# Keys of the first attention turned by 32-by-32 blocks on VectorE after a trip through DRAM

## The chip, the core and the metric

One NeuronCore of one Trainium2 chip runs the whole program. The metric is device microseconds of one execution, as the median of several runs; a profiled execution of the same program gives the trace. In the trace PE is TensorE (matmuls), PEld its weight loads, DVE is VectorE, ACT ScalarE, POOL GpSimd, and SP the engine whose queue issues all DMAs here. L539 is line 539 of the kernel.

## What is computed

One step of a two-layer streaming encoder over 640 rows: 512 rows of a new stream (four row tiles of 128) and 8 running streams with 16 new rows each (the fifth row tile). Only the first mixer, the forgetting attention, is touched:

```python
def fox_mixer(h, q_pos, past, w_in, b_f, w_out):
    proj = h @ w_in
    q, k, v, f_pre, gate = jnp.split(proj, [...], axis=-1)
    ...                                # 16 heads of 64
    logf = jax.nn.log_sigmoid((f_pre + b_f).astype(jnp.float32))
    ...                                # cached keys and values ahead of the new ones
    def block(qb, cqb, pq):
        s = jnp.einsum('bqhd,bkhd->bhqk', qb, k_all).astype(jnp.float32) * FOX_SCALE
        s = s + jnp.moveaxis(cqb, 1, 2)[..., None] - ck
        p = masked_softmax(s, mask).astype(v_all.dtype)
        return jnp.einsum('bhqk,bkhd->bqhd', p, v_all)
    ...
    return o @ w_out, (k, v, logf.astype(h.dtype))
```

The new keys are also outputs, row by row (fox_k_p for the 512 rows, fox_k_s for the 128). For the scores the head dimension has to lie on the partitions, so the keys are needed turned. Products run in a split form: each fp32 operand is a high and a low part (fp32r), and three products stand for one.

## The kernel before

The phases follow one another: first attention (to about 550 us of the span), cross attention, feed-forward, then latent attention, cross attention and feed-forward of the second layer.

In the first attention the 16 heads are worked off in eight pairs, pr = 0 to 7. Each pair's stage merges three lists of steps by their relative position (`merge`, L210): `prompt_list(pr)`, the attention of the 512 rows; `sample_list(pr)`, that of the running streams over their cached keys; and a `fill` list of projections for pairs to come. Keys and values are projected for four heads (two pairs, 256 columns) at a time, so `k_list(g)` with g = 0 to 3 runs four times: g = 0 beside `logf_list` and `q_list(0)` ahead of the first pair, g = 1, 2, 3 as the first part of the fill of pairs 1, 3 and 5, followed there by the out projection of the pair before (`out_list`: ten products of six matmuls of 512 columns, each added into X by VectorE at L332) and by `q_list(pr + 1)`.

`k_list(g)` (L522) loads 256 columns of weights, projects the five row tiles into PSUM (L204), and ScalarE copies each into `krow` (L550). `store` writes `krow` to the two outputs (L531, L532). `tr(j)`, once for each of the two pairs, turns 128 columns: four TensorE transposes into one PSUM bank for the 512 rows (L539), from which `evac_split` makes the high part on ScalarE (L222) and the low part on VectorE (L223), the tiles kT; and one transpose for the 128 rows (L543), which VectorE copies into `kn` (L544). `sample_list` takes from kn the new columns of each stream on POOL (L688). kT is read by the scores of the pair, L627: for a block of query rows six matmuls, two heads of 64 rows by the three products of the split, `qT` stationary.

The cached keys already take another way: `sample_list`'s `load` brings them in blocks (L684: four DMAs of 128 KB, one for each 32 of the 128 columns, in runs of 32 floats, 128 bytes) into `kr`, and VectorE's 32-by-32 block transpose (L692) makes the turned keys out of it.

The order of instructions on each engine's queue is not quite the order of the program. A planner in the framework lays them out when the program is built: by its own estimated times, an instruction whose operands it holds ready may stand ahead of an earlier one that still waits, and otherwise the program's order decides. On the chip each queue then runs strictly in that order. Buffers come from tagged pools: `pw` has four of 128x512 floats (scores, biases), PSUM has three of `mm` (products), two of `s` (scores), two of `t` (transposes), one of `o`; `mrow` has two and serves the memory projection late in the phase.

Of the kernel before, what the change touches and what calls it, by code (L numbers as in the profile page):

```python
# [9 lines left out]
F32 = mybir.dt.float32  # L10
# [8 lines left out]
P = 128  # L19
D = 1024  # L20
KD = D // P
NP = 512
NT = 640
TT = NT // P
# [68 lines left out]
def fox_mla_kernel(ctx: ExitStack, tc: tile.TileContext, I, O):  # L93
    nc = tc.nc
    V, A, G, S, T = nc.vector, nc.scalar, nc.gpsimd, nc.sync, nc.tensor
# [6 lines left out]
    drp = ctx.enter_context(tc.tile_pool(name="drp", bufs=1, space=DRAM))  # L102
# [5 lines left out]
    ident = cst[:, C_ID:C_TRI]  # L108
# [27 lines left out]
    def psum_t():  # L136
        return pat.tile([P, 512], F32, tag="t", name="ps_t", bufs=2)
# [72 lines left out]
    def merge(*lists):  # L210

        steps = [((i + 0.5) / len(l), n, i) for n, l in enumerate(lists) for i in range(len(l))]
        for _, n, i in sorted(steps):
            lists[n][i]()
# [5 lines left out]
    def evac_split(hi, lo, ps, scale=None):  # L220
        if scale is None:
            A.copy(hi, ps)  # L222
            V.tensor_tensor(lo, ps, hi.bitcast(F32), ALU.subtract)  # L223
        else:
            A.activation(hi, ps, AF.Copy, scale=scale)
            V.scalar_tensor_tensor(lo, ps, scale, hi.bitcast(F32), ALU.mult, ALU.subtract)
# [178 lines left out]
    def fox_phase():  # L405
# [8 lines left out]
        with ExitStack() as st:  # L414
# [5 lines left out]
            ckd = drp.tile([NH, NP], F32, name="ckd")  # L420
            csd = drp.tile([P, KS], F32, name="csd")
            lfd = drp.tile([P, NH], F32, name="lfd")
            Qbd = [fp.tile([P, B, 32], F32, name=f"Qbd{i}", bufs=1) for i in range(2)]

            def pw_tile():
# [96 lines left out]
            def k_list(g):  # L522
                c0 = 256 * g
                d = {}

                def load():
                    d["w"] = load_w([(0, 256, w_in[:, 1024 + c0:1024 + c0 + 256])])
                    d["row"] = fp.tile([P, TT, 256], F32, tag="krow", name="krow", bufs=1)

                def store():  # L530
                    S.dma_start(ko[:, :, c0:c0 + 256], d["row"][:, 0:TT - 1, :])  # L531
                    S.dma_start(kso[:, c0:c0 + 256], d["row"][:, TT - 1, :])  # L532

                def tr(j):
                    cs_ = slice(j * P, (j + 1) * P)
                    kT = [fp.tile([P, NP], F32R, tag=f"kT{i}", name=f"kT{i}", bufs=3) for i in range(2)]
                    pt = psum_t()
                    for t in range(TT - 1):
                        T.transpose(out=pt[:, t * P:(t + 1) * P], in_=d["row"][:, t, cs_], identity=ident)  # L539
                    evac_split(kT[0], kT[1], pt)  # L540
                    kn = fp.tile([P, P], F32, tag="kn", name="kn", bufs=3)
                    pt = psum_t()
                    T.transpose(out=pt[:, 0:P], in_=d["row"][:, TT - 1, cs_], identity=ident)  # L543
                    V.tensor_copy(kn, pt[:, 0:P])  # L544
                    ks[2 * g + j] = (kT, kn)

                L = [load]
                for t in range(TT):
                    L += gemm(lambda t=t: as_ops(nx.T, slice(t * P, (t + 1) * P), d["w"], slice(0, 256), KD), 256,
                              lambda ps, t=t: A.copy(d["row"][:, t, :], ps[:, 0:256]), parts=2)  # L550
                return L + [store, lambda: tr(0), lambda: tr(1)]

            def q_list(pr):
                c0 = P * pr
                Q = Qbd[pr % 2]
                d = {}

                def load_q():
                    d["q"] = load_w([(0, P, w_in[:, c0:c0 + P])], per=8)
                    qT = [fp.tile([P, NP], F32R, tag=f"qT{i}", name=f"qT{i}", bufs=2) for i in range(2)]  # L560
                    qs_[pr] = (qT, Q)

                def load_g():
                    d["g"] = load_w([(0, P, w_in[:, 3088 + c0:3088 + c0 + P])], per=8)
                    sg[pr] = fp.tile([P, NT], F32, tag="sig", name="sig", bufs=2)

                def done_q(ps, half):
                    qT = qs_[pr][0]
                    n = HALF if half == 0 else NP - HALF
                    evac_split(qT[0][:, half * HALF:half * HALF + n], qT[1][:, half * HALF:half * HALF + n],  # L570
                               ps[:, 0:n], FOX_SCALE)
                    if half == 1:
                        for hh in range(2):
                            A.activation(Q[64 * hh:64 * hh + 64, :, TS * hh:TS * hh + TS],
                                         ps[64 * hh:64 * hh + 64, n:HALF].rearrange("p (b t) -> p b t", t=TS),
                                         AF.Copy, scale=FOX_SCALE)

                def done_g(ps, half):
                    A.activation(sg[pr][:, half * HALF:(half + 1) * HALF], ps[:, 0:HALF], AF.Exp, scale=-1.0)

                def sig():
                    A.activation(sg[pr], sg[pr], AF.Ln, bias=1.0)
                    A.activation(sg[pr], sg[pr], AF.Exp, scale=-1.0)

                L = []
                for ld, nm, dn in ((load_q, "q", done_q), (load_g, "g", done_g)):
                    L.append(ld)
                    for half in range(2):
                        L += gemm(lambda nm=nm, half=half: ws_ops(d[nm], slice(0, P), nx.T,
                                                                  slice(half * HALF, (half + 1) * HALF), KD),  # L590
                                  HALF, lambda ps, dn=dn, half=half: dn(ps, half), parts=3)
                return L + [sig]
# [198 lines left out]
                    nx.all(t + 1)  # L791
                vl[1 + t]()
            vl[-1]()
            merge(logf_list(), k_list(0) + q_list(0))
            mems = mem_list(0, lambda: fp) + mem_list(1, lambda: fp)
            for pr in range(8):
                fill = []
                if pr % 2 == 1 and pr < 7:
                    fill += k_list(pr // 2 + 1)
                elif pr < 7:  # L800
                    fill += q_list(pr + 1)
                if 0 < pr < 7:
                    ld, tiles = out_list(pr - 1)
                    fill += [ld] + sum(tiles, [])
                if pr % 2 == 1 and pr < 7:
                    fill += q_list(pr + 1)
                if pr % 2 == 0 and pr < 6:
                    fill += v_list(pr // 2 + 1)
                if pr == 6:
                    fill += sum(mems[:4], [])  # L810
                if pr == 7:
                    fill += sum(mems[4:9], [])
                merge(prompt_list(pr), sample_list(pr), fill)
                finish(pr)
# [998 lines left out]
```

## Time and profile before

| | |
|---|---|
| median of three runs | 2077.21 us (2076.77 to 2082.59) |
| the profiled execution | 2078.31 us |
| its span, first to last instruction | 2076.5 us |
| mean granted TensorE clock | 0.996 |
| DMA packets over the span | 352123, 236.37 MB, 133444 of them under 512 bytes |
| TensorE idle in 40 to 360 us of the span | 320.00 - 314.79 = 5.2 us |

The profile page gives the busy share of each engine, the time in 40 slices, the DMA queues, the chain of work that ended last and the costliest groups of instructions. The trace can be asked further: by stretch of time, line or tile, for waits and for single instructions in order of time. A busy share is a mean over stages with different limits, so the page is read first and the stretch with the changed code after it. "Idle before" is the time an engine stood before an instruction, with what released it. Starts of matmuls are closer together than they are long, since they are pipelined.

### The profile page before, as it was taken

How to read it: one execution, taken by the hardware profiler on the slowest of the kernel's cores; microseconds unless marked ns; L12 is line 12 of the kernel's file. 1: busy time of each engine (PE TensorE's matmuls, PEld its weight loads, DVE VectorE, ACT ScalarE, POOL GpSimd, SP SyncE). 2: the span in 40 equal slices, each digit the busy share in tenths (PEclk: the TensorE clock that was granted, in tenths of full speed). 3: DMA queues.
4: the chain of work that ended last, by engine and by line, in shares of the span. 5: the costliest groups of instructions: out<-in, count | busy, mean ns of one | idle time of the engine just before them, and what ended most of it. 6: DMA issues, size and time to landing. Idle time of an engine off the chain costs nothing. (4 is left out here: it accounts for less than half of the span.)

```text
span 2076.5 us, 34659 instructions
## 1 busy us (share of the span) xinstructions
PE 2022.2 (97%) x13501; PEld 1809.6 (87%) x13501; DVE 1390.2 (67%) x2658; ACT 884.8 (43%) x1723; POOL 196.9 (9%) x398
## 2 busy tenths in 40 slices
PE   7999999999999999999999989999999999999998
PEld 7988888877987899999998978887987899999997
DVE  5455555655556896687687567777556886687686
ACT  4443344554343443343344455554343443343342
POOL 1222222220100000000002311100000000000000
PEclk9999999999999999999999999999999999999999
DMA  7565656477557332232221342113566332232221
GB/s 195 117 153 119 154 142 148 144 232 230 139 165 197 103 92 72 82 92 71 82 82 55 103 112 53 53 52 87 132 178 188 97 90 73 82 92 71 82 82 61
DMA packets 352123, 236.37 MB, mean 114 GB/s; under 512 B 133444, under 2 KB 316484, under 8 KB 351960
## 3 DMA queue, kind: packets, MB, share of 16 engines
q1 hardware_dynamic: 351960, 234.16, 40.4%
q8 instruction: 107, 1.75, 0.4%
q14 instruction: 56, 0.46, 0.1%
HBM read 216.90 MB, written 17.21 MB: 113 GB/s over the span
## 5 line engine op out<-in xcount | busy, mean ns | idle before, releaser
L204 PE MATMUL mm<-hT,whi 128*128 128x320 f32 x1744 | 288.6, 312 | 2.9 <-ACT hT L222 2.9
L204 PEld LDWEIGHTS mm<-hT,whi 128*128 128x128 f32 x1744 | 262.2, 190 | 8.4 <-ACT hT L222 4.3
L151 DVE TENSOR_TENSOR wlo<-raw,whi 128x1024 fp32r<-128x1024 f32 (+4 forms) x145 | 170.0, 1175 | 136.0 <-ACT whi L150 115.7
L332 DVE TENSOR_TENSOR X<-mm,X 128x512 f32<-128x512 f32 x270 | 183.0, 686 | 113.5 <-PE mm L204 111.9
L150 ACT CAST whi<-raw 128x1024 fp32r<-128x1024 f32 (+4 forms) x145 | 144.6, 1003 | 133.0 <-PE mm L204 64.9
L1154 ACT CAST whi<-tw 128x512 fp32r<-128x512 f32 (+1 forms) x120 | 91.9, 766 | 214.4 <-PE mm L204 127.8
L204 PE MATMUL mm<-whi,oT 128*128 128x512 f32 x544 | 178.6, 407 | 3.1 <-DVE X L332 1.7
L204 PE MATMUL mm<-whi,aT 128*128 128x512 f32 x560 | 173.0, 390 | 0.3 <-ACT aT L1119 0.3
L204 PE MATMUL mm<-hT,wlo 128*128 128x320 f32 x872 | 155.4, 312 | 0.0
L204 PEld LDWEIGHTS mm<-hT,wlo 128*128 128x128 f32 x872 | 133.5, 190 | 3.3 <-issue 3.2
L232 POOL TENSOR_SCALAR rstd<-ss 128x1 f32<-128x1 f32 x49 | 16.1, 328 | 1252.8 <-ACT hn L230 1248.4
L204 PE MATMUL mm<-s,whi 128*128 128x320 f32 x768 | 128.2, 309 | 0.0
L204 PE MATMUL mm<-whi,hT 128*128 128x256 f32 (+2 forms) x800 | 126.0, 296 | 0.2 <-ACT whi L150 0.2
L204 PEld LDWEIGHTS mm<-whi,aT 128*128 128x128 f32 x560 | 104.4, 188 | 22.5 <-ACT aT L1119 1.2
L204 PEld LDWEIGHTS mm<-whi,oT 128*128 128x128 f32 x544 | 96.7, 189 | 26.9 <-DVE X L332 4.1
L204 PEld LDWEIGHTS mm<-s,whi 128*128 128x128 f32 x768 | 116.6, 188 | 0.0
L1155 DVE TENSOR_TENSOR wlo<-tw,whi 128x512 fp32r<-128x512 f32 (+1 forms) x120 | 103.3, 861 | 19.5 <-ACT whi L1154 19.1
L204 PEld LDWEIGHTS mm<-whi,hT 128*128 128x128 f32 x800 | 109.5, 192 | 3.7 <-issue 1.7
L204 PE MATMUL mm<-wlo,aT 128*128 128x512 f32 x280 | 108.8, 389 | 0.0
L204 PE MATMUL mm<-wlo,oT 128*128 128x512 f32 x272 | 108.3, 401 | 0.0
L1154 ACT CAST whi<-raw 128x1024 fp32r<-128x1024 f32 x44 | 46.3, 1052 | 131.8 <-PE mm L204 70.9
L204 PE MATMUL ps_s<-whi,aT 128*128 128x512 f32 x320 | 98.6, 389 | 0.0
(336 smaller groups left out, 4173.2 us busy)
## 6 DMA issues: line engine op xcount, KB each, us to landing
rawg<-w_ffn_gu SPq DMA_DIRECT2D x80, 512.0 KB, 3.8
raw<-w_ffn_down SPq DMA_DIRECT2D x44, 512.0 KB, 3.7
raw<-w_x_kv SPq DMA_DIRECT2D x32, 512.0 KB, 4.2
vr<-cache_mem_v SPq DMA_DIRECT2D x32, 512.0 KB, 5.5
raw<-w_fox_in SPq DMA_DIRECT2D x30, 512.0 KB, 6.3
kr<-cache_fox_k SPq DMA_DIRECT2D x64, 128.0 KB, 5.2
vr<-cache_fox_v SPq DMA_DIRECT2D x16, 512.0 KB, 5.1
raw<-w_x_q SPq DMA_DIRECT2D x16, 512.0 KB, 6.1
```

Of the source, the lines that this page charges most:

```text
L150: A.copy(hi[:, 0:m], raw[:, 0:m])
L151: V.tensor_tensor(lo[:, 0:m], raw[:, 0:m], hi[:, 0:m].bitcast(F32), ALU.subtract)
L204: T.matmul(st["ps"][:, 0:n], lhsT=l, rhs=r, start=(j == 0), stop=(j == m - 1))
L232: G.tensor_scalar(r, ss, EPS, None, ALU.add)
L332: V.tensor_tensor(xs, ps, xs, ALU.add)
L1154: A.copy(hi[:, o:o + m], src)
L1155: V.tensor_tensor(lo[:, o:o + m], src, hi[:, o:o + m].bitcast(F32), ALU.subtract)
```

## The change

`store` first writes the whole `krow` tile (all five row tiles, 256 columns, 640 KB) to a DRAM tile `kd[g]`, and then the two outputs as before. Two new steps `back(0)` and `back(1)` follow it: for each pair four DMAs of 80 KB bring the keys back into `kraw`, 32 columns to 32 partitions, so that the 32x32 blocks lie as VectorE's block transpose wants them (128-byte runs; the buffers are those of `mrow`). `tr(j)` no longer uses TensorE or PSUM: a block transpose of 128x512 fills `kt`, a tile of the tag `pw`; another of 128x128 fills `kn`; and `evac_split` reads `kt` in SBUF where it read PSUM. `k_list` returns `tr` as a list of its own, which stands behind `q_list(0)` at the beginning, and at the end of the fill in pairs 1, 3 and 5, behind the out projection and `q_list(pr + 1)`; before it stood right behind `store`.

```diff
--- before.py
+++ after.py
@@ -420,6 +420,7 @@
             ckd = drp.tile([NH, NP], F32, name="ckd")
             csd = drp.tile([P, KS], F32, name="csd")
             lfd = drp.tile([P, NH], F32, name="lfd")
+            kd = [drp.tile([NT, 256], F32, name=f"kd{g}") for g in range(4)]
             Qbd = [fp.tile([P, B, 32], F32, name=f"Qbd{i}", bufs=1) for i in range(2)]
 
             def pw_tile():
@@ -528,27 +529,32 @@
                     d["row"] = fp.tile([P, TT, 256], F32, tag="krow", name="krow", bufs=1)
 
                 def store():
+                    S.dma_start(kd[g].rearrange("(t p) n -> p t n", p=P), d["row"])
                     S.dma_start(ko[:, :, c0:c0 + 256], d["row"][:, 0:TT - 1, :])
                     S.dma_start(kso[:, c0:c0 + 256], d["row"][:, TT - 1, :])
 
+                def back(j):
+
+                    r = d["raw", j] = fp.tile([P, NT // 32, 32], F32, tag="mrow", name="kraw", bufs=2)
+                    src = kd[g].rearrange("(m j) n -> j m n", j=32)
+                    for i in range(4):
+                        o = j * P + 32 * i
+                        S.dma_start(r[32 * i:32 * i + 32], src[:, :, o:o + 32])
+
                 def tr(j):
-                    cs_ = slice(j * P, (j + 1) * P)
                     kT = [fp.tile([P, NP], F32R, tag=f"kT{i}", name=f"kT{i}", bufs=3) for i in range(2)]
-                    pt = psum_t()
-                    for t in range(TT - 1):
-                        T.transpose(out=pt[:, t * P:(t + 1) * P], in_=d["row"][:, t, cs_], identity=ident)
-                    evac_split(kT[0], kT[1], pt)
                     kn = fp.tile([P, P], F32, tag="kn", name="kn", bufs=3)
-                    pt = psum_t()
-                    T.transpose(out=pt[:, 0:P], in_=d["row"][:, TT - 1, cs_], identity=ident)
-                    V.tensor_copy(kn, pt[:, 0:P])
+                    kt = fp.tile([P, NP], F32, tag="pw", name="kt", bufs=4)
+                    V.transpose(kt, d["raw", j][:, 0:NP // 32].rearrange("p m x -> p (m x)"))
+                    V.transpose(kn, d["raw", j][:, NP // 32:].rearrange("p m x -> p (m x)"))
+                    evac_split(kT[0], kT[1], kt)
                     ks[2 * g + j] = (kT, kn)
 
                 L = [load]
                 for t in range(TT):
                     L += gemm(lambda t=t: as_ops(nx.T, slice(t * P, (t + 1) * P), d["w"], slice(0, 256), KD), 256,
                               lambda ps, t=t: A.copy(d["row"][:, t, :], ps[:, 0:256]), parts=2)
-                return L + [store, lambda: tr(0), lambda: tr(1)]
+                return L + [store, lambda: back(0), lambda: back(1)], [lambda: tr(0), lambda: tr(1)]
 
             def q_list(pr):
                 c0 = P * pr
@@ -791,12 +797,14 @@
                     nx.all(t + 1)
                 vl[1 + t]()
             vl[-1]()
-            merge(logf_list(), k_list(0) + q_list(0))
+            kl, kt = k_list(0)
+            merge(logf_list(), kl + q_list(0) + kt)
             mems = mem_list(0, lambda: fp) + mem_list(1, lambda: fp)
             for pr in range(8):
-                fill = []
+                fill, kt = [], []
                 if pr % 2 == 1 and pr < 7:
-                    fill += k_list(pr // 2 + 1)
+                    kl, kt = k_list(pr // 2 + 1)
+                    fill += kl
                 elif pr < 7:
                     fill += q_list(pr + 1)
                 if 0 < pr < 7:
@@ -804,6 +812,7 @@
                     fill += [ld] + sum(tiles, [])
                 if pr % 2 == 1 and pr < 7:
                     fill += q_list(pr + 1)
+                fill += kt
                 if pr % 2 == 0 and pr < 6:
                     fill += v_list(pr // 2 + 1)
                 if pr == 6:
```

## Rows read from the trace of the kernel before

**Rows 1.** The page, part 1: busy us (share) x instructions

```profile
PE 2022.2 (97%) x13501; PEld 1809.6 (87%) x13501; DVE 1390.2 (67%) x2658; ACT 884.8 (43%) x1723; POOL 196.9 (9%) x398
```

**Rows 2.** Windows: us; busy us (x) of PE, PEld, DVE, ACT, POOL; PEclk; DMA share; GB/s

```profile
40.00:360.00 320.00, 314.79 (x2582) 275.96 (x2581) 175.27 (x450) 129.72 (x291) 77.77 (x162) 1.00 0.60 141
```

**Rows 3.** Windows around and behind the key transposes of two stages

```profile
120.00:135.00 15.00, 15.00 (x101) 11.76 (x100) 12.16 (x30) 7.12 (x16) 1.52 (x5) 1.00 0.70 160
134.00:145.00 11.00, 11.00 (x88) 8.52 (x87) 8.70 (x24) 3.20 (x7) 6.07 (x15) 1.00 0.79 138
235.00:246.00 11.00, 11.00 (x82) 8.46 (x82) 9.05 (x23) 2.78 (x7) 6.09 (x15) 1.00 0.36 47
```

**Rows 4.** Timeline of TensorE, second key stage: start, us, operation, count

```profile
...
125.94 0.66 PE L539 MATMUL ps_t<-cst,krow 128*128 128x128 f32 x4
126.43 0.27 PE L543 MATMUL ps_t<-cst,krow 128*128 128x128 f32 x1
126.46 0.48 PE L204 MATMUL mm<-wlo,oT 128*128 128x512 f32 x1
126.87 0.61 PE L627 MATMUL ps_s<-kT,qT 64*128 64x384 f32 x3
127.42 0.66 PE L539 MATMUL ps_t<-cst,krow 128*128 128x128 f32 x4
128.01 0.43 PE L627 MATMUL ps_s<-kT,qT 64*128 64x384 f32 x1
128.37 0.33 PE L543 MATMUL ps_t<-cst,krow 128*128 128x128 f32 x1
128.63 0.44 PE L627 MATMUL ps_s<-kT,qT 64*128 64x384 f32 x2
...
```

**Rows 5.** Timeline of TensorE, the same scores one pair later

```profile
...
175.94 0.79 PE L627 MATMUL ps_s<-kT,qT 64*128 64x384 f32 x6
...
```

**Rows 6.** Timeline of TensorE, first key stage; idle before and releaser in brackets

```profile
...
47.29 0.60 PE L539 MATMUL ps_t<-cst,krow 128*128 128x128 f32 x4
...
49.36 0.33 PE L543 MATMUL ps_t<-cst,krow 128*128 128x128 f32 x1 [0.89 <-ACT krow L550]
...
```

**Rows 7.** Groups by line and form, VectorE, 40 to 360 us: busy, mean ns

```profile
L692 DVE STREAM_TRANSPOSE KT<-kr 128x512 f32<-128x512 f32 x28 | 18.9, 692 | 0.0
...
L223 DVE TENSOR_TENSOR kT<-ps_t,kT 128x512 fp32r<-128x512 f32 x8 | 5.5, 690 | 0.9 <-ACT kT L222 0.8
...
L544 DVE COPY kn<-ps_t 128x128 f32<-128x128 f32 x8 | 2.3, 282 | 0.7 <-PE ps_t L543 0.7
```

**Rows 8.** DMA issues, 40 to 360 us: count, KB each, median us to landing

```profile
...
raw<-w_fox_in SPq DMA_DIRECT2D x26, 512.0 KB, 6.3
kr<-cache_fox_k SPq DMA_DIRECT2D x60, 128.0 KB, 5.3
...
out_fox_v_p<-vsb SPq DMA_DIRECT2D x3, 512.0 KB, 4.2
...
```

**Rows 9.** Timeline of SP behind the store of the second stage: start, us

```profile
...
125.66 0.37 SPq L532 DMA_DIRECT2D out_fox_k_s<-krow  x1
...
127.53 0.41 SPq L148 DMA_DIRECT2D raw<-w_fox_in  x1
...
131.22 5.04 SPq L684 DMA_DIRECT2D kr<-cache_fox_k  x4
...
```

**Rows 10.** Timeline of TensorE: first scores of the first and third pair

```profile
...
70.73 0.96 PE L627 MATMUL ps_s<-kT,qT 64*128 64x512 f32 x6
...
165.77 0.97 PE L627 MATMUL ps_s<-kT,qT 64*128 64x512 f32 x6
...
```

**Rows 11.** Timeline of ScalarE: a cast of weights after the second stage

```profile
...
139.69 1.05 ACT L150 CAST whi<-raw 128x1024 fp32r<-128x1024 f32 x1 [0.45 <-ACT pw L720]
...
```

**Rows 12.** Waits, 40 to 360 us: who for whom, us in total, times, longest

```profile
DVE jk L701 <- DMA pw<-csd: 10.1, 6, 2.8
...
PEld mm L204 <- DVE X L332: 3.8, 6, 1.7
...
```

## The prediction

> **What bounds the kernel now.** I read the page first, then the stretches of the first attention, then each engine there. The page shows TensorE busy for 97% of the span, VectorE for 67%, ScalarE for 43% [rows 1]. So the time is the length of TensorE's queue, and an edit is worth what it takes out of that queue, less what it makes TensorE wait. The reader is then to look at the stretch in which the changed code runs: from 40 to 360 us TensorE is busy for 314.79 of 320 us at the full granted clock, VectorE for 175.27 [rows 2]. TensorE's idle time there is 5.2 us in all. VectorE's mean share of 55% misleads: in the 15 us around the key transposes it is busy for 12.16 us, and in the 11 us behind them for 8.70 to 9.05 us, both some 80% [rows 3].
>
> **What is removed: TensorE.** Each of four key stages loses ten 128x128 transposes through PSUM. They are pipelined, so the price is not their duration but the distance between starts. In the second stage five of them lie between 125.94 and 126.46, four between 127.42 and 128.01, one between 128.37 and 128.63 [rows 4]: 0.52 + 0.59 + 0.26 = 1.37 us. That is the low bound. They also cut the six score matmuls of line 627 in pieces. That line issues two heads on 64 rows each, and where nothing splits the six (the same key block of the next pair) they last 0.79 us [rows 5]. Here they run from 126.87 to 129.07 (128.63 + 0.44), 2.20 us, with five transposes among them: 1.41 us to be won. With the 0.52 us ahead of them that is 1.93 us, and the same pattern stands at three stages (its starts 125.94, 227.7 and 328.8 us): 5.8 us. In the first stage nothing splits scores: nine transposes at 0.52 / 5 = 0.104 us each, 0.94 us, and one that waits 0.89 us for the last copy of the key rows [rows 6]: 1.8 us. **Gross gain 7.6 us**, low bound 1.8 + 3 x 1.37 = 5.9 us.
>
> **What is added: VectorE and ScalarE.** A 128x512 block transpose costs 692 ns (the cached keys already go that way). The small one has no row: the 128x128 copy that it replaces takes 282 ns, and I take the same, with 0.69 us as the upper end and somewhat under the copy as the lower. The subtraction keeps its 690 ns [rows 7]; its source and ScalarE's move from PSUM to SBUF, which I price at zero, within 0.1 us either way. So VectorE gets 2 x 0.69 = 1.4 us more per stage. More important is where it stands: before, 2 x (0.28 + 0.69) = 1.9 us of key work lay around 127 to 129.6 us; now 2 x (0.69 + 0.28 + 0.69) = 3.3 us lie some 8 to 15 us later, where VectorE has about 2 us free of 11 [rows 3].
> The Trainium skill speaks against the swap: VectorE: DVE Perf Modes, section Rules for kernel authors, says to transpose 128x128 on TensorE where a PSUM destination will do. By its section The three transpose paths (390 ns on TensorE, 311 ns on VectorE for 128x128 in bf16) a block costs about alike on either; this trace's distance between starts makes TensorE the cheaper engine, but also shows it to be the full one. By that rule the change loses, in the way of the slower rival below.
>
> **What is added: the way through DRAM.** Per stage SP issues one more write of 640 KB and eight reads of 80 KB in runs of 128 bytes. The nearest rows: a 512 KB write lands 4.2 us after its issue, a 128 KB read of cached keys in runs of the same 128 bytes after 5.3 us [rows 8]. Four such reads hold SP for 5.04 us where the queue is full; at the 0.41 us of a single load they would take 1.6 [rows 9]. The write waits for the fifth copy of the rows, as line 532 does at 125.66. So the first half is back at 125.7 + 4.2 + (1.6 to 5.0) + 5.3 = 137 to 140 us, the second at 138 to 145. The keys are needed at 165.77 us [rows 10]; block transpose, cast and subtraction behind the read are some 2 us (an estimate, three times the 0.69 of [rows 7]). That leaves 18 us of cover: TensorE does not wait for the keys themselves. The first stage is tighter: write at 49.4 (the last copy frees the transpose at 49.36, [rows 6]), landed 53.6, first half back between 60.5 and 64, keys ready by 66, needed at 70.73 [rows 10] less the 1.8 us saved, 68.9. Cover 3 us; beyond it each us late is a us lost, once.
> **What queues on SP behind these.** The reads wait for the write, and all that stands behind them on SP waits too: a load of weights (127.53) and the cached keys of the next pair (131.22) [rows 9], and around these the bias row csd and the broadcast ckb. The weights need 6.3 us [rows 8] and land by 133.8; their cast starts at 139.69, and not on a DMA [rows 11]: 6 us of cover against 3 to 6 us of delay. Price zero, at most 2 us. The DMA engines are 0.60 busy at 141 GB/s [rows 2], 235 GB/s if full; 1.31 MB more per stage of some 50 us is 5.6 us, a share near 0.7: enough left.
> Here the Trainium skill warns too: DMA: Bandwidth & Descriptors, section Specifications, wants at least 512 bytes per descriptor for line rate and tells of a read-modify-write below that. No sum here hangs on it; by [rows 8] the 128-byte reads of a quarter of the size land hardly sooner than the loads of 512 KB, so the trace agrees that they are dear by the byte.
> **The one new wait** is VectorE's: the block transpose stands in its in-order queue at the place that the planner gave it, by the planner's idea of the round trip. Where the reads land later, all behind it waits: the adds into X of line 332 that free the PSUM buffers of the out projection, the evacuations of the queries, the softmax of the samples; and TensorE waits for those. The nearest row: VectorE waits at line 701 for a row out of DRAM six times, 10.1 us in all, 1.7 each, 2.8 at most; in the same stretch the weight loads of TensorE wait 3.8 us for the adds [rows 12]. I take one wait of 1.7 us for each of the eight halves, 13.6 us of VectorE's time, and let a fifth pass to TensorE (three PSUM buffers lie between): 2.7 us. Ends: 0, all covered, and 13.6 us, all passed on.
> At nothing: the kt tile holds one of four pw buffers for some 2 us late in a stage, when the pair's score tiles are done with theirs; POOL gets its copies of kn later, but is idle for 242 of 320 us [rows 2]; PSUM's t buffers are relieved.
>
> **The sum.** 7.6 - 2.7 = 4.9 us. The profiled execution took 2078.31 us (span 2076.5); it becomes 2073.4. The median of the runs lies 1.1 us below it, 2077.21, so I forecast 2072.3 us. Bounds of the terms: 2077.2 - 7.6 = 2069.6 and 2077.2 - 5.9 + 13.6 = 2084.9 us.
>
> **Rivals.**
> *Clean win.* VectorE never stands: the full 7.6 us, 2069.6 us. For it: 1.9 us of VectorE's work leave the worst place, and a new order can also win part of the 5.2 us of idle time, down to about 2066. Against it: VectorE's 80%.
> *A new wait takes it all.* TensorE's queue is shorter, but TensorE waits for adds or softmax as much as it gained (1 us per half), or the 40 transposes filled time in which it would have waited anyway: 2077 us. Against the latter: no other wait stands near them, and the split scores visibly take longer.
> *Slower.* VectorE stands for the round trip, not for the rest of one. If the transposes stand at about 134 us in its queue and the reads land at 140 to 145, it waits 6 to 11 us; less 2.8 us that the buffers may cover (the longest wait of [rows 12], under which TensorE stayed 98% busy), TensorE loses 3 to 8 us in each of four stages, 12 to 32 us against 7.6: 2082 to 2102, about 2092. It decides from a wait of (7.6 + 6.2) / 4 + 2.8 = 6.3 us per stage on. For it: two trips follow one another where [rows 12] shows one. Against: VectorE is itself late there behind TensorE, and the planner counts both trips.
>
> **How the numbers follow.** A comparison of this kernel can tell about 0.3%, 6.2 us, from no change: faster means under 2071.0, slower over 2083.4. Forecast case 0.50 (2072.3, its own range 2068 to 2076; 0.20 of it faster, 0.30 same); clean win 0.20, faster; a new wait takes it all 0.16, same; slower 0.14. Sums: faster 0.40, same 0.46, slower 0.14. For 8 in 10 the range takes in the clean win with the idle time and the case of no change, and ends at the edge of the slower rival: 2066 to 2081.
>
> **What would show each step.** The six score matmuls of line 627 unsplit at 0.79 us in the second, fourth and sixth pair. Wrong in the cover: TensorE idle before line 627 at 69 us. Wrong in the main term: VectorE idle with the raw key tile's DMA as releaser for over 6 us per stage, and TensorE waiting for the adds of line 332 for much more than now. Wrong on SP: casts of weights waiting for their DMA at 140 us. The prediction falls if the stretch from 40 to 360 us does not get 2 to 8 us shorter, or if the phases behind it change by more than 2 us.

## The result, and the profile after

The changed kernel takes 2108.96 us (median of four runs, 2105.60 to 2110.26) against 2077.18 (2076.77 to 2082.59): 1.0144 times as long, interval 1.0123 to 1.0165. It is 31.8 us slower; forecast were 2072.3 us with a range of 2066 to 2081. The rival "slower", 2082 to 2102, names the right side, but the time lies above its range too, and the cause is, as will be seen, another. The profiled execution took 2110.26 us (span 2108.2).

Part 1 of the page of the changed kernel: TensorE is still the bound, with about the same share as in [rows 1], and its busy time has grown by 13.6 us though 40 transposes were taken from it.

```profile
PE 2035.8 (97%) x13461; PEld 1816.8 (86%) x13461; DVE 1395.0 (66%) x2666; ACT 883.4 (42%) x1723; POOL 190.0 (9%) x398
```

So look at stages. The end of a pair is where ScalarE starts its cast of the pair's output (L766, after L772):

| | pair 0 ends at | pairs 1, 3, 5 (with a key stage) | pairs 2, 4 | pair 6 | pair 7 | rest of the program |
|---|---|---|---|---|---|---|
| before | 109.9 us | 49.6, 49.6, 49.9 | 52.2, 51.5 | 71.2 | 62.8 | 1579.9 |
| after, difference | +9.1 | -1.7, -0.9, -1.2 | +2.9, +1.1 | +6.1 | +9.0 | +7.3 |

The stages in which the transposes went did get shorter. The loss is in other stages, 22 us of it from pair 6 on, where no new key is projected or fetched back. The windows of TensorE show it as two things. First the changed kernel (columns as in [rows 2]; the two stretches to the end of pair 5, then pair 6, pair 7, and the tail of the phase):

```profile
40.00:118.80 78.80, 74.01 (x568) 64.97 (x567) 31.24 (x78) 28.55 (x61) 15.27 (x34) 0.94 0.60 137
118.80:371.70 252.90, 247.79 (x2012) 216.68 (x2011) 146.27 (x378) 99.15 (x230) 51.59 (x118) 0.98 0.58 136
371.70:449.00 77.30, 71.28 (x427) 56.52 (x426) 43.41 (x88) 33.54 (x62) 20.29 (x36) 0.96 0.66 188
449.00:520.80 71.80, 65.01 (x373) 49.23 (x372) 38.22 (x77) 34.64 (x60) 10.06 (x19) 0.95 0.71 232
520.80:575.00 54.20, 47.70 (x252) 40.80 (x252) 31.59 (x40) 24.49 (x39) 8.02 (x13) 0.97 0.52 157
```

and the same stretches of the kernel before:

```profile
40.00:109.70 69.70, 67.67 (x574) 63.05 (x573) 30.80 (x78) 27.79 (x61) 15.07 (x34) 1.00 0.60 142
109.70:362.40 252.70, 249.51 (x2034) 214.94 (x2032) 145.20 (x376) 102.98 (x231) 62.70 (x128) 1.00 0.61 142
362.40:433.60 71.20, 70.68 (x450) 57.40 (x449) 42.51 (x86) 34.87 (x64) 16.22 (x28) 1.00 0.52 168
433.60:496.40 62.80, 59.27 (x360) 45.61 (x360) 37.22 (x73) 33.22 (x59) 10.53 (x17) 0.97 0.66 222
496.40:543.30 46.90, 45.85 (x256) 40.29 (x255) 31.29 (x39) 23.61 (x39) 8.49 (x13) 1.00 0.60 170
```

Idle is length less PE busy: 4.8 + 5.1 + 6.0 + 6.8 + 6.5 = 29.2 us against 2.0 + 3.2 + 0.5 + 3.5 + 1.0 = 10.3, so 18.9 us more. Granted clock (first number behind the engines): 0.94 over 78.8 us gives away 4.7 us of full-speed work; with 5.1, 3.1, 3.6 and 1.6 us from the other rows that is 18 us, against 1.9 before: 16 us more, with some 3 us of rounding. Idle and clock, 35 us, less 6 us for the transposes (below) come near the 31.8. About half of the loss is thus not waiting, but slower running behind waits.

What answers [rows 4] and [rows 7]: the six scores in the second key stage stand unsplit, as expected, and the durations on VectorE are close to those assumed (0.70 and 0.74 us, assumed 0.69; the small transpose 0.27, below, assumed 0.28). TensorE's timeline, then VectorE's groups in 40 to 360 us:

```profile
135.32 0.79 PE L633 MATMUL ps_s<-kT,qT 64*128 64x384 f32 x6
```

```profile
L548 DVE STREAM_TRANSPOSE kt<-kraw 128x512 f32<-128x512 f32 x7 | 4.9, 704 | 0.0
...
L223 DVE TENSOR_TENSOR kT<-kt,kT 128x512 fp32r<-128x512 f32 x6 | 4.4, 741 | 1.2 <-ACT kT L222 1.0
```

The last column, 0.0, is the idle time ahead of the block transposes: VectorE never stood for the trip. The write landed sooner than the 4.2 us forecast, a read about as forecast, 5.3 us (issues, count, KB, median us to landing; [rows 8] before):

```profile
raw<-w_fox_in SPq DMA_DIRECT2D x26, 512.0 KB, 4.6
...
kd<-krow SPq DMA_DIRECT2D x4, 640.0 KB, 3.5
kraw<-kd SPq DMA_DIRECT2D x32, 80.0 KB, 5.6
```

**The first stage.** VectorE, POOL and TensorE in the changed kernel's timeline, three fences (start, us, operation, idle before and releaser):

```profile
69.43 0.49 DVE L226 SCALAR_TENSOR_TENSOR qT<-mm,qT 128x320 fp32r<-128x320 f32 x1 [4.93 <-ACT qT L225]
69.84 0.70 DVE L548 STREAM_TRANSPOSE kt<-kraw 128x512 f32<-128x512 f32 x1
...
75.27 0.27 DVE L549 STREAM_TRANSPOSE kn<-kraw 128x128 f32<-128x128 f32 x1
...
77.24 0.69 DVE L640 CUSTOM_DVE_ANT_0 pw<-ps_s,pw 128x512 f32<-128x512 f32 x1 [0.18 <-POOL pw L625]
```

```profile
70.80 0.41 POOL L694 COPY KT<-kn 128x64 f32<-128x64 f32 x2 [47.69 <-DVE kn L549]
75.60 0.24 POOL L694 COPY KT<-kn 128x64 f32<-128x64 f32 x1 [4.39 <-DMA raw<-w_fox_in]
75.83 0.69 POOL L624 TENSOR_SCALAR pw<-ckb,cq 128x512 f32<-128x512 f32 x1
```

```profile
72.82 1.15 PE L204 MATMUL mm<-hT,wlo 128*128 128x320 f32 x6
78.00 0.79 PE L633 MATMUL ps_s<-kT,qT 64*128 64x384 f32 x3 [4.03 <-DVE nm L640]
...
80.23 1.12 PE L656 MATMUL ps_t<-cst,pw 128*128 128x128 f32 x4
```

The keys were in SBUF by some 61 us: the DMA engines are idle from 61.2 to 65 us. But the block transposes stand on VectorE behind evacuations of the queries, which wait for TensorE. So kn comes at 70.7 and 75.5 us; POOL stands at its copy of kn (in the second row the trace names a weight load that had long landed; it is kn at 75.27 + 0.27), and behind that copy, in order, the bias tile of the first scores (75.83, before at 62.22). The softmax waits for the bias, PSUM is not freed, TensorE stands for 4.0 us, and then runs slowly: four transposes of 128x128 in 1.12 us, where [rows 4] has 0.66.

**SP.** Its timeline behind the second key stage, after:

```profile
137.65 8.99 SPq L542 DMA_DIRECT2D kraw<-kd  x8
...
147.24 3.66 SPq L690 DMA_DIRECT2D kr<-cache_fox_k  x3
161.63 0.39 SPq L692 DMA_DIRECT2D vr<-cache_fox_v  x1
162.06 1.06 SPq L608 DMA_DIRECT2D ckb<-ckd  x2
...
167.79 0.84 SPq L692 DMA_DIRECT2D vr<-cache_fox_v  x1
168.72 0.81 SPq L148 DMA_DIRECT2D raw<-w_fox_in  x1
169.62 1.20 SPq L148 DMA_DIRECT2D raw<-w_fox_out  x1
```

and before, the rows beside those of [rows 9]:

```profile
128.60 2.57 SPq L602 DMA_DIRECT2D ckb<-ckd  x2
...
136.36 0.79 SPq L148 DMA_DIRECT2D raw<-w_fox_in  x1
142.48 0.35 SPq L148 DMA_DIRECT2D raw<-w_fox_out  x1
...
153.11 1.03 SPq L686 DMA_DIRECT2D vr<-cache_fox_v  x2
154.25 1.03 SPq L148 DMA_DIRECT2D raw<-w_fox_in  x1
```

In both kernels SP stands for vr, the load of a pair's cached values, whose buffers come free only when TensorE has done the sample values of the running pair (L686, after L692). Before, the next pair's ckb, most of its kr (cached keys) and its weights stand ahead of that wait. After, most stand behind it: they go out from 162 us on, 5 us ahead of the end of pair 1 and behind it (166.9 us), where the kernel before has them out 5 to 31 us ahead (its pair ends at 159.5). SP's waits for this reason in 40 to 560 us (us in total, times, longest), after, 8.8 us each:

```profile
SPq L692 <- PE ps_o L746: 52.9, 6, 15.7
```

and before, 3.5 us each:

```profile
SPq L686 <- PE ps_o L740: 35.4, 10, 9.5
```

### The profile page after: what moved, and what is told of

It reads as the page before. It is cut to its first block, busy times and chain, and to the rows that moved or that the text cites. A ratio compares the mean times of both kernels' runs of the same rounds, so it can differ in the third digit from the quotient of the medians.

```text
span 2108.2 us, 34589 instructions
## 1 busy us (share of the span) xinstructions
PE 2035.8 (97%) x13461; PEld 1816.8 (86%) x13461; DVE 1395.0 (66%) x2666; ACT 883.4 (42%) x1723; POOL 190.0 (9%) x398
## 5 line engine op out<-in xcount | busy, mean ns | idle before, releaser
L232 POOL TENSOR_SCALAR rstd<-ss 128x1 f32<-128x1 f32 x49 | 16.7, 341 | 1276.0 <-ACT hn L230 1271.5
L1164 DVE TENSOR_TENSOR wlo<-tw,whi 128x512 fp32r<-128x512 f32 (+1 forms) x120 | 103.5, 863 | 18.9 <-ACT whi L1163 16.2
```

The costliest lines, as they stand in the source:

```text
L232: G.tensor_scalar(r, ss, EPS, None, ALU.add)
L1164: V.tensor_tensor(lo[:, o:o + m], src, hi[:, o:o + m].bitcast(F32), ALU.subtract)
```

## The experiments

The theories: **P**, the new place of `tr` (keys late, POOL standing at kn). **D**, the nine DMAs of a stage. **S**, kt taking slots of pw. **W**, VectorE standing for the trip, the rival on record. Two more, **Q** (the order of SP's queue) and **B** (the bytes or the short runs), come with e5. All times are medians; before beside them measured 2077.2 to 2079.3 us.

### The change taken apart: e1 to e4

e1_pe_late:

```diff
-                return L + [store, lambda: tr(0), lambda: tr(1)]
+                return L + [store], [lambda: tr(0), lambda: tr(1)]
```

> The kernel before with one thing of the change: the TensorE transposes of the keys, with their evacuations, stand at the end of the stage's fill, where the changed kernel has its block transposes. No trip through DRAM, no block transpose, no kt tile. Theory P (place: the keys come late, and POOL stands at its copy of kn ahead of the bias tiles, so the loss comes with the place alone): 2090 to 2110 us, TensorE waiting at the first scores of the first pair (L627 for L634). Theory D (the nine DMAs of a stage push the other loads on SP): no loss, 2075 to 2080. Theory S (the kt tile takes a slot of the ring pw from the next pair's bias tiles): no loss, 2075 to 2080. Theory W (VectorE stands for the round trip, the slower rival on record): no loss, 2075 to 2080.

Measured 2071.13 us, 0.9966 [0.9954, 0.9979]: **faster than both kernels**. P falls as the main cause. Its kn is as late as 65.8 us, but there the planner has put the first bias tiles ahead of the copies on POOL (57.58 us). So a late key costs nothing by itself; what stands behind it on POOL may make it dear.

e2_dma_only (kernel before):

```diff
+                    S.dma_start(kd[g].rearrange("(t p) n -> p t n", p=P), d["row"])
...
-                return L + [store, lambda: tr(0), lambda: tr(1)]
+                return L + [store, lambda: back(0), lambda: back(1), lambda: tr(0), lambda: tr(1)]
```

> The kernel before with the write of the key rows to DRAM and the eight reads back added in every stage; nobody uses what is read back, the keys are transposed on TensorE at the old place. Theory D (the DMAs and what they push on SP cost the time): 2095 to 2110 us. Theories P, S and W: within 0.3% of before, 2073 to 2083, since no place, slot or wait of VectorE is changed.

Measured 2107.95 us, 1.0144 [1.0128, 1.0159]: the whole loss, from DMAs whose data nobody uses. Its pair 0 ends 4.3 us late, pair 2 takes 3.1 us more, pairs 6 and 7 take 6.8 and 7.1 more, and SP's timeline has the pattern of the changed kernel:

```profile
132.83 7.62 SPq L542 DMA_DIRECT2D kraw<-kd  x8
...
141.05 4.05 SPq L694 DMA_DIRECT2D kr<-cache_fox_k  x3
158.13 0.38 SPq L696 DMA_DIRECT2D vr<-cache_fox_v  x1
158.56 1.05 SPq L612 DMA_DIRECT2D ckb<-ckd  x2
```

e3_tr_early (changed kernel):

```diff
-                return L + [store, lambda: back(0), lambda: back(1)], [lambda: tr(0), lambda: tr(1)]
+                return L + [store, lambda: back(0), lambda: back(1), lambda: tr(0), lambda: tr(1)], []
```

> The changed kernel with its block transposes put back to the old place in the list of steps, right behind the reads. Theory P: the loss goes, 2070 to 2085 us. Theory W: the loss grows, since VectorE then meets the block transposes before the reads have landed and stands for most of a 12 us trip four times: 2115 to 2140 us. Theory D: as the changed kernel, 2105 to 2113. Theory S: as the changed kernel or little less, 2100 to 2113, since kt still takes slots of pw.

Measured 2113.38 us, 1.0167 [1.0152, 1.0183]. P falls again; W too: even in this place VectorE's waits name no DMA of kraw, and the loss grows by 4 us, not by 6 to 31.

e4_kt_own (changed kernel): kt in the raw tile.

```diff
-                    kt = fp.tile([P, NP], F32, tag="pw", name="kt", bufs=4)
+                    V.transpose(kn, raw[:, NP:NT])
+                    kt = raw[:, NP:2 * NP]
+                    V.transpose(kt, raw[:, 0:NP])
```

> The changed kernel, but kt lies in the free end of the raw tile (the block transpose of kn goes first and clears the place) and no longer in the ring pw of the bias and probability tiles. Theory S: most of the loss goes, 2075 to 2090 us, and the bias tiles of the first scores of an even pair run a stage ahead again. Theory P: as the changed kernel less 0 to 8 us, 2100 to 2110. Theories D and W: as the changed kernel, 2105 to 2113.

Measured 2102.80 us, 1.0121 [1.0106, 1.0136]: 6 us back, S is at most a fifth. Only D is left.

### Bytes, or the queue that issues them: e5 to e8

e5_dma_act (e2 with):

```diff
-                        S.dma_start(r[32 * i:32 * i + 32], src[:, :, o:o + 32])
+                        A.dma_start(r[32 * i:32 * i + 32], src[:, :, o:o + 32])
```

(the write to kd likewise)

> The kernel of e2_dma_only (before, plus the write and the eight reads of each key stage, unused), with these nine DMAs issued by ScalarE's queue and not by SP's. Same bytes, same 128-byte runs, same moment. Theory Q (nine more instructions on SP's in-order queue put the next pair's loads behind a load that waits for TensorE): the loss of 30 us goes, 2073 to 2085 us, and ckb of an even pair is issued some 30 us ahead of its stage again, not 5. Theory B (the bytes or the 128-byte runs crowd the DMA engines): the loss stays, 2100 to 2110 us.

Measured 2081.87 us, 1.0018 [1.0009, 1.0027]: the same bytes in the same runs cost 4 us in place of 30. Theory B is refuted, Q holds in the time. Its second sign came only in part: ckb of an even pair goes out at 147.0 us, 16 us ahead of its stage, not some 30.

e6_two_reads (e2 with two reads of 320 KB on SP):

```diff
+                    src = kd[g].rearrange("(p q) n -> p (q n)", p=P)
+                    S.dma_start(r, src[:, j * NT:(j + 1) * NT])
```

> The kernel of e2_dma_only with the eight reads of a stage (32 partitions, 128-byte runs) replaced by two reads of the same 640 KB in runs of 2560 bytes, still on SP's queue. Theory Q: three more instructions on SP in place of nine leave most of the order alone, 2073 to 2088 us. Theory B in its form by bytes: 2100 to 2110 us; in its form by short runs: 2073 to 2083 us, which e5_dma_act then tells from theory Q.

Measured 2077.73 us, 1.0001 [0.9992, 1.0011]. No loss.

e7_after_act (changed kernel, write and reads on ScalarE's queue, edited as in e5):

> The changed kernel with its write and reads on ScalarE's queue in place of SP's, nothing else. Theory Q: what is left is the place (6.6 us won in e1_pe_late) and the transposes taken from TensorE, so 2062 to 2078 us. Theory B, and the theories S (slot of pw) and W (VectorE stands for the round trip): 2095 to 2110 us. The first stage stays as tight as in the changed kernel, some 4 to 9 us of loss there, if POOL's stand at KT<-kn (L694) has its own cause.

Measured 2076.17 us, 0.9991 [0.9981, 1.0000]. 33 us come back with SP's queue alone. Pair 0 still ends 3.1 us late. ScalarE pays: its timeline shows it standing while its queue issues the eight reads.

```profile
132.92 10.44 ACTq L542 DMA_DIRECT2D kraw<-kd  x8
143.40 0.48 ACT L663 COPY PT<-ps_t 128x384 f32<-128x384 f32 x1 [10.84 <-DMA kraw<-kd]
```

e8_dma_ckb_ahead (e2 with):

```diff
+                    fill = prompt_list(pr + 1, True) + fill
```

(the `load` of `prompt_list` alone; it is taken out of the next pair's own list)

> The kernel of e2_dma_only with the two ckb loads of the next pair moved one stage ahead by hand, first in the stage's fill, so that they can't fall behind the vr load that waits for TensorE. If the late ckb (and with it POOL's bias tiles) is what costs the time: pairs 2 and 4 get their 3 us back each, 2085 to 2100 us in all, the rest of the loss (pairs 6, 7 and the tail) standing with other late loads. If ckb is only one of many late loads: 2102 to 2110 us. Theory B: no change from e2_dma_only, 2105 to 2110 us.

Measured 2112.06 us, 1.0164 [1.0149, 1.0179]. ckb now goes out at 141.5 us, ahead of vr, and nothing is won: ckb is not the load that matters. e7 points the same way: there ckb goes out behind vr, at 160.4 us and 1.8 us ahead of its stage, without a loss.

### The engine alone: e9, e10, e12

e9_no_trip_late and e10_no_trip_early (changed kernel without the trip, and so without the exchange of the 32-row groups; `tr` at the new and at the old place):

```diff
-                    V.transpose(kt, d["raw", j][:, 0:NP // 32].rearrange("p m x -> p (m x)"))
+                    V.transpose(kt.rearrange("p (t n) -> p t n", n=P), d["row"][:, 0:TT - 1, j * P:(j + 1) * P])
```

> The changed kernel without the trip: VectorE's block transposes read the key rows straight from SBUF, at the changed kernel's late place, and no write to DRAM and no read back is issued. It leaves out the exchange of the 32-row groups, so the keys it computes with are not the right ones; every other instruction is that of the change. Beside e1_pe_late (2071.1 us, the same place with TensorE's transposes) it prices the swap of the engine alone. If TensorE's queue length sets the time, as in the forecast: 5.9 to 7.6 us less, 2063.5 to 2065.5 us. If the transposes on TensorE filled time in which it waits anyway: 2069 to 2073 us. If VectorE's extra work delays what TensorE waits for: over 2073 us. Beside the changed kernel (2109.0 us) the rest is the price of the trip.

Measured 2067.83 us, 0.9949 [0.9931, 0.9967].

> As e9_no_trip_late, at the old place behind the store: the exchange of the 32-row groups is left out here too. Beside the kernel before (2077.2 us) it prices the engine alone, with nothing moved. By the forecast's gross gain: 2069.6 to 2071.3 us. If TensorE's transposes cost nothing: 2075 to 2079 us. If the 6.6 us of e1_pe_late came from the new place and not from a chance of the order, this one is slower than e9_no_trip_late by some 5 us.

Measured 2071.83 us, 0.9972 [0.9963, 0.9981]. With nothing moved, 40 transposes fewer on TensorE are worth 6.0 us; the late place gives 4.0 us more. Against e9 the trip costs 41 us on SP (2108.96) and 8 us on ScalarE's queue (e7); the 41 are 11 more than e2's 30, and the runs do not say where these come from. And the late place with VectorE is 3.3 us better than with TensorE (e1), less than the 5.9 expected. The 4.0 and the 3.3 are rough: the four runs of e9 lie between 2065.3 and 2071.1 us.

e12_act_own (e7 and e4 together):

> The changed kernel with the trip on ScalarE's queue (e7_after_act, 2076.2 us) and kt in the free end of the raw tile (e4_kt_own, which won 6 us against the changed kernel). If the slot of pw costs time of its own: 2068 to 2073 us. If it only cost because everything was late: 2074 to 2078 us.

Measured 2081.12 us, 1.0013 [1.0003, 1.0022]: 5 us slower than e7, where the same edit won 6 us in e4. Every edit makes the planner lay out all queues anew, so 4 to 6 us between two kernels of this kind can be the new order and not the edit. This holds for e4, e12 and the 4 us of e5 and e17, and is a caution on e1 and e10 too.

### What it is in SP's queue: e11, e13 to e18

e11_after_vr_act (changed kernel) and e15_dma_vr_act (e2):

```diff
-                    S.dma_start(d["vr", bq], cv[:, 8 * bq:8 * bq + 8, pr * P:(pr + 1) * P])
+                    A.dma_start(d["vr", bq], cv[:, 8 * bq:8 * bq + 8, pr * P:(pr + 1) * P])
```

> The changed kernel with the loads of vr (two of 512 KB in each pair, which wait until TensorE has done the sample values of the pair before) on ScalarE's queue in place of SP's; the nine DMAs of the trip stay on SP. Theory Q in its exact form (what stands behind vr on SP is what comes late): most of the loss goes, 2072 to 2088 us, with ckb and the weights issued ahead of their stage. If the number of SP's instructions as such is the matter: 2100 to 2112 us. ScalarE's queue may stand for vr instead, which would leave 5 to 15 us of the loss.

Measured 2098.10 us, 1.0100 [1.0085, 1.0115]: 11 of 32 us.

> The kernel of e2_dma_only with the vr loads on ScalarE's queue; the nine DMAs stay on SP. If SP's stand for vr is all of the mechanism: 2077 to 2088 us. If it is a third, as in e11_after_vr_act: 2095 to 2100 us. If nothing: 2105 to 2112 us.

Measured 2090.33 us, 1.0062 [1.0047, 1.0078]: 18 of 30 us. With vr gone from SP, its pairs 1 to 5 take 248.7 us together, less than the 252.7 before; what stays is pair 0 (7.6 us late) and the tail. So the stand for vr is the largest single link that was tested, not the whole.

e13_tiny_reads (e2 with):

```diff
+                        S.dma_start(r[32 * i:32 * i + 32, 0:1], src[:, 0:1, o:o + 32])
```

> The kernel of e2_dma_only with the eight reads of a stage cut to one 128-byte run for each partition (4 KB a read instead of 80 KB); nine more DMAs on SP as there, nobody uses what is read. If the number of DMAs on SP is the matter: as e2_dma_only, 2100 to 2110 us. If the size of the reads (their time on SP and in the DMA engines) puts the others back: 2076 to 2085 us. Between: both.

Measured 2078.09 us, 1.0000 [0.9990, 1.0009]. Not the number of DMAs.

e17_eight_long (e2 with eight reads of 80 KB in long runs):

```diff
+                        S.dma_start(r[32 * i:32 * i + 32], src[32 * i:32 * i + 32, j * NT:(j + 1) * NT])
```

> The kernel of e2_dma_only with its eight reads of 80 KB in runs of 2560 bytes in place of 128 bytes (32 partitions each, as there). If the 128-byte runs make the reads dear: 2076 to 2082 us, as e6_two_reads. If the eight pieces of 80 KB on SP do it, whatever their runs: 2100 to 2110 us.

Measured 2082.63 us, 1.0022 [1.0012, 1.0031]. It is the pair "eight pieces in short runs" that costs 30 us; either part alone costs 5 us or nothing. But in the trace long runs hardly relieve SP. Its timeline in e17:

```profile
130.43 6.55 SPq L540 DMA_DIRECT2D kraw<-kd  x8
...
141.34 2.20 SPq L610 DMA_DIRECT2D ckb<-ckd  x2
...
155.91 0.38 SPq L694 DMA_DIRECT2D vr<-cache_fox_v  x1
```

The reads hold SP for 6.55 us, against 7.62 in e2, and land after 5.2 us (median), against 5.1. One us of SP's time does not make 25 us. What differs is the order behind them: ckb stands ahead of vr here, behind it in e2, and the first weights of the memory projection go out 1.5 us ahead of the end of pair 5, in e2 16.7 us behind it. That the order makes the 25 us is the reading that is left, not a test; ckb's place alone does not (e8).

e14_dma_mem_ahead (e2 with the first fetch of the memory's gain and rows in pair 5's fill):

```diff
+                if pr == 5:
+                    fill = [mems[0][0].fetch] + fill
```

> The kernel of e2_dma_only with the first loads of the memory (gain g_mem and the first 128 rows) put by hand into the stage of pair 5, where the kernel before has them by itself (286 and 314 us; e2_dma_only has them at 374 us). If the late memory rows carry the loss of pairs 6, 7 and the tail: 10 to 21 us come back, 2087 to 2098 us. If not: 2103 to 2112 us.

Measured 2104.16 us, 1.0128 [1.0109, 1.0147]: 4 us back, in the band of "not". Pairs 6 and 7 take 3.8 and 3.3 us less than in e2, but pair 0, which the edit does not touch, ends 2.9 us later: early memory rows help a little.

e16_dma_mem_vr (both):

> e14_dma_mem_ahead and e15_dma_vr_act in one kernel. If the two late loads are the whole chain, their gains add and the kernel comes to 2077 to 2086 us. If something else on SP (the weights behind the reads) holds the rest: 2088 to 2100 us.

Measured 2086.28 us, 1.0041 [1.0027, 1.0054]: the gains add, 22 of 30 us; 9 us remain, and pair 0 ends 8.0 us late.

In the traces of all kernels one figure goes with the loss: when SP issues the first weights of the memory projection, against the end of pair 5. Before, e1, e5 to e7, e9, e10, e12, e13, e17: 1.5 to 11 us ahead, at most 5 us lost. e11, e15, e16: 5 to 7 us behind, 9 to 21 us lost. After, e2 to e4, e8, e14: 12 to 20 us behind, 25 to 36 us lost. The last run asks whether it is a cause.

e18_dma_kv_ahead (e2 with):

```diff
+                if pr == 5:
+                    fill += mems[1][:1]
```

> The kernel of e2_dma_only (2108.0 us) with the first load of the memory projection's weights (w_x_kv) put by hand at the end of pair 5's fill, so that SP issues it some 30 us ahead of the end of that stage in place of 17 us behind it. If this late load is the cause of what pairs 6, 7 and the tail lose (21 us): 2087 to 2098 us. If it is only a mark of a queue that is late as a whole: 2103 to 2112 us; a weight buffer that is held longer may even cost some us more.

Measured 2106.06 us, 1.0129 [1.0112, 1.0146]. The load goes out at 341.7 us, 32 us ahead; pair 6 is 7.8 us shorter than in e2 and no longer than before, pair 7 is 5.8 us longer, and pair 0, which the edit does not touch, ends 3.7 us later. So pair 6 did wait for this load, but for the phase it is a mark of a queue that is late as a whole: a load put ahead by hand passes most of the lateness on.

## Why the prediction was wrong, and where it was right

**The gross gain was right in kind.** Forecast 7.6 us with 5.9 as low bound; e10 measures 6.0, interval 3.9 to 7.7. The shorter key stages (1.7, 0.9 and 1.2 us) show it less clearly, since they carry other losses. The Trainium skill (VectorE: DVE Perf Modes, Rules for kernel authors) would keep these transposes on TensorE. Here TensorE is the full engine, and the swap of the engine alone wins 6.0 us in e10. But e10 leaves out the exchange of the 32-row groups; with it, the best run of the whole swap is e7, 1.7 us better than before, which is hardly more than nothing. So no run here decides against the rule.

**The new wait of VectorE (2.7 us, bounds 0 to 13.6) was not there**, and the cover of 18 us behind the trip held. The rival "slower" had the sign and a middle of 2092 us, but its mechanism, VectorE standing 6 to 11 us for the trip, is absent in the changed kernel and in e3, where the place invited it.

**The step that failed is the price of what queues on SP: "Price zero, at most 2 us". It measured 30 us (e2).** I named the weights, kr, csd and ckb, but not vr. And I held one of them, a weight load, against its cover [rows 9, 11] and moved the others by 3 to 6 us in the same order. The order itself changed. The text before the prediction says that the planner lays out each queue by its own estimates; I used this for VectorE's wait alone. What the trace of before did show, and I did not ask, is that SP stands at vr for TensorE ten times, 35.4 us in all and up to 9.5 us, with the next pair's loads just ahead of it: a load that comes to stand behind such a wait can be late by that much. My own sign for this fired: ScalarE's casts wait for the weights w_fox_in 5.7 us in all in 40 to 371 us, before 1.5:

```profile
144.03 1.05 ACT L150 CAST whi<-raw 128x1024 fp32r<-128x1024 f32 x1 [2.83 <-DMA raw<-w_fox_in]
```

The two signs by which the prediction was to fall came too: up to the end of pair 5 the kernel got 9.3 us longer, not 2 to 8 us shorter, and behind it 22 us longer.

Late, in pairs 6, 7 and the tail, the waits reach TensorE (us in total, times, longest, 372 to 575 us, after). The first, for the memory's rows hn, was 0.5 us before; the others, for the adds into X and for casts of weights, are not on the list of before:

```profile
PE ps_t L246 <- DVE hn L238: 3.9, 2, 3.1
PE mm L204 <- DVE X L332: 3.5, 2, 3.0
PE mm L388 <- ACT whi L150: 2.5, 4, 1.3
```

**POOL's copies of kn "at nothing" failed in the first stage, for a part.** "Idle for 242 of 320 us" is a mean; what counts is what stands behind the copy in order, the first bias tile. Pair 0 loses 9.1 us in the changed kernel; e4 has the same stand on POOL (47.1 us) and loses 7.5 us there, and in e9, where the same copy comes at 51 us, pair 0 ends as before. But e2, where it comes at 51 us too, loses 4.3 us there: its load of ckb goes out behind the eight reads (64.65 us, before 58.54), and POOL waits for that.

```profile
68.71 0.69 POOL L628 TENSOR_SCALAR pw<-ckb,cq 128x512 f32<-128x512 f32 x1 [12.58 <-DMA ckb<-ckd]
```

So some 5 of the 9 us are left for the stand at kn, and that split was not tested.

**kt in pw at nothing** stays open: minus 6 us in e4, plus 5 in e12.

**The clock had no term.** I priced waits one for one; in the changed kernel about half of the loss is half-speed running behind them. In e2, with the same loss, it is about a third: from 40 to 575 us the granted clock is 0.98 there, 0.96 in the changed kernel, 1.00 before.

**The place of tr had no term either**, and gives 4.0 us (e9 against e10) to 6.6 us (e1), both near the 4 to 6 us that two builds can differ by.

The Trainium skill's warning on descriptors under 512 bytes (DMA: Bandwidth & Descriptors, Specifications) pointed at these reads, and the same reads in long runs lose 25 us less (e17); but landing and SP's time hardly differ, so in this case the trace doesn't show the rule's reason, only an order that differs. The prediction's remark that short runs are dear by the byte is not borne out by these reads.

What stays open: by which of its estimates the planner puts vr ahead of the other loads for these reads, which the trace can't show; and the 9 us that e16 leaves. Of these 8.0 lie in pair 0, where ckb goes out behind the eight reads at 67.4 us (before 58.5); but in e13 the first bias tile comes as late as in e2 (68.7 us) and pair 0 loses nothing, so this link is not shown. The same order with shorter reads was not tried.

## What to carry to other kernels

A DMA added to a queue that issues all loads is priced by what it does to the order of that queue: find the queue's long waits for the engine that it feeds in the trace, see which loads stand just ahead of it, and ask what happens if they come to stand behind; if that is dear, put the new DMAs on another queue or make them few and long, and test with the DMAs alone, unused, before anything is built on them. Where an engine seems idle enough for a step that comes later, look at the next instruction behind that step on its queue, not at the busy share. And where a planner lays out the queues, a difference of 5 us between two builds proves little by itself; here the simplest half of the change, the old transposes at the new place (2071.1 us), was better than the whole.

## What the hardware showed that was not expected

A wait of TensorE can cost more than its length. In the changed kernel TensorE does nothing from 74 to 78 us; the granted clock is 1.00 before, and in the stretch behind the wait it is 0.50 (1.2 of 2.4 GHz), with TensorE busy for 9.45 of 10 us; later it is 1.00 again:

```profile
60.00:74.00 14.00, 13.97 (x90) 12.31 (x88) 3.16 (x7) 3.41 (x6) 0.41 (x2) 1.00 0.63 126
74.00:78.00 4.00, 0.01 (x1) 0.01 (x1) 2.88 (x6) 1.52 (x5) 2.32 (x5) 1.00 0.34 87
79.00:89.00 10.00, 9.45 (x31) 4.16 (x31) 6.19 (x18) 3.77 (x9) 1.87 (x5) 0.50 0.37 96
89.00:110.00 21.00, 21.00 (x181) 19.98 (x181) 10.91 (x35) 10.36 (x25) 6.88 (x14) 1.00 0.59 131
```

Ten us at half speed do the work of five, so this wait of 4 us cost about 9, which is what pair 0 lost. Second, an engine whose queue issues DMAs pays for it with its own work: eight reads of 80 KB held ScalarE for 10.4 us, as they held SP for 9.0.
